# Issuing the loads and stores of the prepared weight sums from GpSimd, each load behind a copy from the newest low half of weights

## The chip, the cores and the metric

The kernel runs on one core of one Trainium2 chip. The metric is the device time of one execution in microseconds (us); the figure used is the median of several executions.

## The reference

One transformer layer on 256 tokens of width 2048, in fp32. Three attention branches are gated and mixed, then comes a feed-forward part, then a small gated input. Cut to what matters here:

```python
S, D = 256, 2048;  D_FF = 5632
z = split_cols(h @ w_in)                       # queries, keys, values, index queries, gates
o_fox = fox_attention(...)                     # 6 heads, forget-gated
o_nsa = nsa_attention(...)                     # 4 heads: compressed + selected blocks + window
o_dsa = dsa_attention(...)                     # 6 heads: an indexer picks 64 keys per query
g_fox, g_nsa, g_dsa = split(sigmoid(z['gate']), 3)
mixed = g_fox * (o_fox @ w_br_fox) + g_nsa * (o_nsa @ w_br_nsa) + g_dsa * (o_dsa @ w_br_dsa)
h = layer_norm(ALPHA * h + mixed @ w_out)
a, b = split(h @ w_ffn_in, 2)
h = layer_norm(ALPHA * h + (silu(a) * b) @ w_ffn_out)
h = h + (p @ w_ple_in) * sigmoid(h @ w_ple_gate)
```

## The kernel before

**Products in halves.** Each fp32 matrix is split into a high and a low half of a shorter type, and a product is three matmuls on TensorE: high by high, low by high, high by low (L244 to L246 in `gemm`; L297 to L299 in `pair_gemm`). `halves` (L156) makes the two: ScalarE writes the high half, VectorE subtracts it from the source and writes the low half. For weights the rows read `whi<-raw` and `wlo<-raw,whi`.

**Weight groups.** `gemm` streams a weight matrix in groups of up to 128x1024 elements (512 KB). SyncE issues the load of a group into one of three `raw` buffers, ScalarE and VectorE split it, TensorE uses it. Each instruction of these engines stands in an order of its own engine that is fixed when the program is built; an engine works through that order and waits at each row for what the row needs. `newest[0]` is, while the program is written down, the low half of the group written last.

**The attention stage** (0 to about 400 us) is written as the projections `c1` to `c7` and `f0` to `f5` of the input, 105 weight groups, with the small work of the heads between them. After each group `tick()` advances a few generators by a step: the heads (`dsa_head`, `nsa_head`, `fox_head`), the indexer (`index_scores`; its sums on VectorE are L744), and others. A step of a head is for instance `rope` (L542 to L546, on VectorE: tiles `ra` and `rb`), whose result TensorE transposes (`sc<-ident,ra`, L553), or `softmax` (L559 to L579): scores on TensorE, maximum on VectorE (L565), exponential on ScalarE (L567), reciprocal and scaling by VectorE (L570, L572, L574, tile `p`), transposition by TensorE (`sc<-ident,p`, L578). A scheduler then sets each engine's order from this program and its dependencies, so what is written between two groups need not stand between the same two.

**The prepared sums.** In the feed-forward product, `pair_gemm` replaces eight products of 2x2 blocks by seven, which takes sums of weight blocks. For seven pieces of the weight (two rows of tiles each), these sums are made early, in the attention stage, by `prepare` (L889 to L920), and kept in DRAM tiles `pre`, already split into halves. A piece ("job") takes two loads of 512 KB (tiles `preb` and `prea`, L898), four subtractions of 128x512 on VectorE (L900 to L904, tile `pret`), four splits into halves (L156), and five stores (L912, L913, L920). `pair_gemm` reads the tiles back from 928 us on. `prepare` runs on the ticks too, as three generators:

```python
PREPARED, PREPARE_FROM = (((4, 2), (5, 2)), ((6, 2), (7, 2), (8, 2)), ((9, 2), (10, 2))), 26
```

The first starts at tick 26 and takes one job there and one at tick 44; the other two start when the compressed values are done, and take two jobs at tick 57, two at 75 and one at 93. These five times are called batch 1 to 5 here: one, one, two, two and one jobs. The `yield 6` between the loads and the first subtraction leaves six ticks. The buffers of the three generators come from the pools `k4`, `gp` and `ka`, which the heads use as well.

**Queues.** All loads of weights and all loads and stores of `prepare` are issued by SyncE, in its order. GpSimd has 44 instructions: some copies and memsets (`blk`, L694, among them) and the loads of the norm parameters (`gb`, L1086). Its copies of one or two elements `...<-wlo` (L511, L1084) write a corner of a tile that is about to be loaded, so that the load cannot be issued before a given low half exists.

Of the kernel before, what the change touches and what calls it, by code (L numbers as in the profile page):

```python
# [10 lines left out]
F32 = mybir.dt.float32  # L11
# [117 lines left out]
def build(ctx: ExitStack, tc: tile.TileContext, A: dict):  # L129
    nc = tc.nc  # L130
    PE, DVE, ACT, POOL = nc.tensor, nc.vector, nc.scalar, nc.gpsimd
# [22 lines left out]
    def halves(src, hi, lo):  # L154

        split_last[:] = [ACT.activation(hi, src, AF.Copy).ins, DVE.tensor_sub(lo, src, hi.bitcast(F32)).ins]  # L156
# [18 lines left out]
    side, beside, now, newest = [], [], [0], [None]  # L175
# [285 lines left out]
    with ExitStack() as at:  # L461
# [429 lines left out]
        def prepare(jobs, pool, tag, after=None):  # L891

            while after and not T[after]["done"]:
                yield 1
            for c, p in jobs:
                rb, ra, t = (pool.tile([P, 2, 512], F32, name=f"pre{x}", tag=tag) for x in "bat")
                for r, n in ((rb, 11 + c), (ra, c)):
                    nc.sync.dma_start(r, A["ffn_in"][n][:, 2 * p:2 * p + 2, :])  # L898
                yield 6
                DVE.tensor_sub(t[:, 0, :], rb[:, 0, :], rb[:, 1, :])  # L900
                DVE.tensor_sub(t[:, 1, :], rb[:, 0, :], ra[:, 0, :])
                yield 1
                DVE.tensor_sub(rb[:, 1, :], rb[:, 1, :], t[:, 1, :])
                DVE.tensor_sub(ra[:, 1, :], ra[:, 1, :], rb[:, 1, :])  # L904
                yield 1
                for i, r in enumerate((rb, ra)):
                    halves(t[:, i, :], r[:, 0, :].bitcast(F32R), t[:, i, :].bitcast(F32R))
                    yield 1
                yield 1
                d = prepared.setdefault(c, {})[p] = dram.tile([P, 8, 512], F32, name="pre")  # L910
                for i, r in enumerate((rb, ra)):
                    nc.sync.dma_start(d[:, i:i + 1, :], r[:, 0:1, :])  # L912
                nc.sync.dma_start(d[:, 2:4, :], t)  # L913
                yield 3
                for r in (rb, ra):
                    halves(r[:, 1, :], r[:, 0, :].bitcast(F32R), r[:, 1, :].bitcast(F32R))
                    yield 1
                yield 1
                for i, r in enumerate((rb, ra)):
                    nc.sync.dma_start(d[:, 4 + 2 * i:6 + 2 * i, :], r)  # L920
                yield 1

        T = {}
        beside.append({"gen": prepare(PREPARED[0], k4, "k4"), "at": PREPARE_FROM})
        lf_task = add(later_load())
        ps = chunk("c1", x=X_first, sizes=[[1], [1]])
# [21 lines left out]
        for i, (pool, tag) in enumerate(((gp, "g"), (ka, "ka"))):  # L948
            beside.append({"gen": prepare(PREPARED[1 + i], pool, tag, "v"), "at": 0})
# [432 lines left out]
```

## Time and profile before

| | |
|---|---|
| median of 3 runs | 1564.12 us (1563.99 to 1565.78) |
| profiled execution | 1562.82 us, of which the span of its instructions 1560.9 us |
| TensorE matmul (PE) | 1545.5 us busy, 99% of the span |
| VectorE (DVE) | 1367.2 us, 88% |
| ScalarE (ACT) | 881.8 us, 56% |
| GpSimd (POOL) | 20.1 us, 1% |
| granted TensorE clock | full throughout |
| DMA | 360.91 MB, 231 GB/s over the span |

In the rows of the trace, PE is TensorE's matmuls, PEld its weight loads, DVE VectorE, ACT ScalarE, POOL GpSimd and SP SyncE. A row of the order of time has the start and the length of an instruction or a run of equal ones in us, the engine, the line, the operation, the tiles written and read (`out<-in`), the shape and the count; in brackets stands the idle time before it and what ended it. A row of waits has engine, tile and line that waited, what it waited for, then the idle time, the number of times and the longest. Rows of a tile have the instruction's duration in ns (smallest, median, largest) and the first and last start in us; the row under it the time from a DMA's issue to its landing.

### The profile page before, as it was taken

To read this page: it belongs to the slowest core of one execution; us is meant where nothing else is said; L and a number is where in the kernel's file an instruction comes from. 1 tells how busy PE (TensorE), PEld (TensorE's weight loads), DVE (VectorE), ACT (ScalarE), POOL (GpSimd) and SP (SyncE) were. 2 spreads that over 40 slices of the span, in tenths; PEclk is the share of its full clock that TensorE was granted. 3 is DMA by queue.
4 is the path that set the end of the run, shared out by engine and by line. 5 is a ranking of instruction groups with operands and counts; after the bars stand their busy time and mean duration, and the time that the engine had idled before them with its cause. 6 is when DMAs were issued, how large, how long until landed. Compare 5 with 4: busy or idle time off the path is not lost. (4 is left out here: it accounts for less than half of the span.)

```text
span 1560.9 us, 20529 instructions
## 1 busy us (share of the span) xinstructions
PE 1545.5 (99%) x7314; PEld 1286.8 (82%) x7314; DVE 1367.2 (88%) x1914; ACT 881.8 (56%) x1155; POOL 20.1 (1%) x44
## 2 busy tenths in 40 slices
PE   9999999999999999999999999999999999999998
PEld 7778899998888888888788888888888888887887
DVE  6779787559898998998879999999999999989896
ACT  5545566556565555544455566656565666555463
POOL 1000000000000000001000000000000000010000
PEclk9999999999999999999999999999999999999999
DMA  8866988566645664658566667777777776886554
GB/s 284 303 215 211 302 284 283 169 209 206 237 158 192 216 236 158 229 172 265 160 219 214 229 213 245 262 263 271 266 261 275 245 267 229 290 289 251 166 171 135
DMA packets 105574, 360.91 MB, mean 231 GB/s; under 512 B 12032, under 2 KB 13184, under 8 KB 105472
## 3 DMA queue, kind: packets, MB, share of 16 engines
q1 hardware_dynamic: 104192, 355.41, 67.2%
q0 software_dynamic: 1280, 4.20, 0.9%
q8 instruction: 57, 0.93, 0.2%
q14 instruction: 45, 0.37, 0.1%
HBM read 337.54 MB, written 22.02 MB: 230 GB/s over the span
## 5 line engine op out<-in xcount | busy, mean ns | idle before, releaser
L156 DVE TENSOR_TENSOR wlo<-raw,whi 128x1024 fp32r<-128x1024 f32 (+3 forms) x539 | 586.7, 1104 | 131.8 <-ACT whi L156 128.0
L156 ACT ACTIVATE whi<-raw 128x1024 fp32r<-128x1024 f32 (+3 forms) x539 | 507.5, 962 | 338.3 <-PE acc L245 99.5
L244 PE MATMUL acc<-whi,k4h 128*128 128x512 f32 (+3 forms) x724 | 274.2, 379 | 1.8 <-ACT k4h L156 1.5
L246 PE MATMUL acc<-wlo,k4h 128*128 128x512 f32 (+3 forms) x724 | 267.0, 370 | 1.1 <-DVE wlo L156 1.1
L245 PE MATMUL acc<-whi,k4l 128*128 128x512 f32 (+3 forms) x724 | 267.2, 369 | 0.6 <-DVE k4l L156 0.6
L156 ACT ACTIVATE wthi<-raw 128x1024 fp32r<-128x1024 f32 x168 | 177.8, 1060 | 149.7 <-DVE raw L380 80.8
L156 DVE TENSOR_TENSOR wtlo<-raw,wthi 128x1024 fp32r<-128x1024 f32 x168 | 202.7, 1219 | 0.0
L297 PE MATMUL sc<-whi,k4h 128*128 128x512 f32 x489 | 191.6, 392 | 0.0
L298 PE MATMUL sc<-whi,k4l 128*128 128x512 f32 x489 | 190.5, 390 | 0.0
L299 PE MATMUL sc<-wlo,k4h 128*128 128x512 f32 x489 | 190.2, 390 | 0.1
L297 PE MATMUL acc<-whi,k4h 128*128 128x512 f32 x401 | 157.4, 393 | 0.3 <-ACT whi L156 0.3
L299 PE MATMUL acc<-wlo,k4h 128*128 128x512 f32 x401 | 156.4, 390 | 0.9 <-DVE wlo L156 0.9
L244 PEld LDWEIGHTS acc<-whi,k4h 128*128 128x128 f32 x724 | 136.1, 188 | 25.7 <-issue 4.7
L298 PE MATMUL acc<-whi,k4l 128*128 128x512 f32 x401 | 156.1, 389 | 0.0
L246 PEld LDWEIGHTS acc<-wlo,k4h 128*128 128x128 f32 x724 | 135.9, 188 | 21.5 <-DVE wlo L156 3.0
L245 PEld LDWEIGHTS acc<-whi,k4l 128*128 128x128 f32 x724 | 136.3, 188 | 18.7 <-DVE k4l L156 1.3
L380 DVE TENSOR_TENSOR raw<-raw 128x1024 f32<-128x1024 f32 x79 | 96.3, 1220 | 14.5 <-DMA raw<-ffn_out 5.9
L299 PEld LDWEIGHTS sc<-wlo,k4h 128*128 128x128 f32 x489 | 91.8, 188 | 19.9 <-DVE wlo L156 0.5
L297 PEld LDWEIGHTS sc<-whi,k4h 128*128 128x128 f32 x489 | 91.9, 188 | 18.8
L298 PEld LDWEIGHTS sc<-whi,k4l 128*128 128x128 f32 x489 | 91.8, 188 | 18.8
L299 PEld LDWEIGHTS acc<-wlo,k4h 128*128 128x128 f32 x401 | 75.2, 188 | 17.6 <-DVE wlo L156 1.9
L297 PEld LDWEIGHTS acc<-whi,k4h 128*128 128x128 f32 x401 | 75.3, 188 | 15.8 <-ACT whi L156 0.7
(370 smaller groups left out, 2120.4 us busy)
## 6 DMA issues: line engine op xcount, KB each, us to landing
raw<-ffn_in SPq DMA_DIRECT2D x169, 512.0 KB, 4.6
raw<-gate SPq DMA_DIRECT2D x96, 512.0 KB, 4.5
raw<-ffn_out SPq DMA_DIRECT2D x88, 512.0 KB, 5.0
raw<-att_c SPq DMA_DIRECT2D x40, 512.0 KB, 4.7
raw<-att_f SPq DMA_DIRECT2D x48, 384.0 KB, 3.8
raw<-ple_gate SPq DMA_DIRECT2D x32, 512.0 KB, 4.2
g<-actd SPq DMA_DIRECT2D x20, 512.0 KB, 5.0
g<-cmp SPq DMA_DIRECT2D x16, 512.0 KB, 5.6
```

The costliest lines, as they stand in the source:

```text
L156: split_last[:] = [ACT.activation(hi, src, AF.Copy).ins, DVE.tensor_sub(lo, src, hi.bitcast(F32)).ins]
L244: PE.matmul(o, xh[:, c], h, start=(k == 0), stop=False)
L245: PE.matmul(o, xl[:, c], h, start=False, stop=False)
L246: PE.matmul(o, xh[:, c], l, start=False, stop=(k == kt - 1))
L297: PE.matmul(o, xh, h, start=first, stop=False)
L298: PE.matmul(o, xl, h, start=False, stop=False)
L299: PE.matmul(o, xh, l, start=False, stop=stop)
L380: DVE.tensor_tensor(t[0], raw[:, 0:1, :].broadcast_to([P, 2, 512]), raw[:, 1:3, :], op=ALU.subtract)
```

## The change

Each of the two loads of a job gets a copy of one element ahead of it on GpSimd: from the low half of the newest weight group into the corner of the tile to be loaded. The loads (L899 after the change) and the five stores (L913, L914, L921) are issued by GpSimd instead of SyncE. In the new file all lines from there on are one higher: the subtractions are L901 to L905.

```diff
             for c, p in jobs:
                 rb, ra, t = (pool.tile([P, 2, 512], F32, name=f"pre{x}", tag=tag) for x in "bat")
                 for r, n in ((rb, 11 + c), (ra, c)):
-                    nc.sync.dma_start(r, A["ffn_in"][n][:, 2 * p:2 * p + 2, :])
+                    POOL.tensor_copy(r[:1, 0, :1], newest[0].bitcast(F32)[:1, :1])
+                    nc.gpsimd.dma_start(r, A["ffn_in"][n][:, 2 * p:2 * p + 2, :])
                 yield 6
...
                 for i, r in enumerate((rb, ra)):
-                    nc.sync.dma_start(d[:, i:i + 1, :], r[:, 0:1, :])
-                nc.sync.dma_start(d[:, 2:4, :], t)
+                    nc.gpsimd.dma_start(d[:, i:i + 1, :], r[:, 0:1, :])
+                nc.gpsimd.dma_start(d[:, 2:4, :], t)
...
                 for i, r in enumerate((rb, ra)):
-                    nc.sync.dma_start(d[:, 4 + 2 * i:6 + 2 * i, :], r)
+                    nc.gpsimd.dma_start(d[:, 4 + 2 * i:6 + 2 * i, :], r)
                 yield 1
```

The scheduler orders each engine anew. On GpSimd, the rows between the corner copies of the constants and those of the norm parameters were, before:

```order
L511 COPY peT<-wlo 1x1
L511 COPY cmp_113<-wlo 1x1
L694 MEMSET blk_853 128x32x17
L694 MEMSET blk_1524 128x32x17
L1084 COPY gb<-wlo 1x2 x4
L1086 DMA gb<-ln_g 128x512
```

After the change the first batch reads (`preb` and `prea` are the two loaded tiles, `pret` the third, `pre` the tile in DRAM):

```order
L511 COPY cmp_113<-wlo 1x1
L898 COPY preb<-wlo 1x1
L898 COPY prea<-wlo 1x1
L899 DMA preb<-ffn_in 128x1024
L899 DMA prea<-ffn_in 128x1024
L913 DMA pre<-preb 128x512
L913 DMA pre<-prea 128x512
L694 MEMSET blk_855 128x32x17
L914 DMA pre<-pret 128x1024
L921 DMA pre<-preb 128x1024
L921 DMA pre<-prea 128x1024
```

The first memset now stands between the stores of batch 1. The other batches follow in the same pattern, in batches 3 and 4 with four copies, then four loads. The copies of the five batches read the low halves of weight groups 26, 44, 57, 75 and 93, counted from the first.

On VectorE, at the end of weight group 27 of the attention stage (batch 1), the order was, before, with the preparation's last low halves of this batch already behind it:

```order
L744 SCALAR_TENSOR_TENSOR work<-ri,zs,work 128x128
L744 SCALAR_TENSOR_TENSOR work<-ri,zs,work 128x256
L744 SCALAR_TENSOR_TENSOR work<-ri,zs,work 128x128
L744 SCALAR_TENSOR_TENSOR work<-ri,zs,work 128x256
L156 TENSOR_TENSOR wlo<-raw,whi 128x1024
```

and after:

```order
L744 SCALAR_TENSOR_TENSOR work<-ri,zs,work 128x128
L744 SCALAR_TENSOR_TENSOR work<-ri,zs,work 128x256
L901 TENSOR_TENSOR pret<-preb 128x512
L902 TENSOR_TENSOR pret<-preb,prea 128x512
L904 TENSOR_TENSOR preb<-preb,pret 128x512
L156 TENSOR_TENSOR wlo<-raw,whi 128x1024
```

The subtractions of batch 1 moved from groups 13 to 22 to groups 27 to 30, one group behind the low half that their loads' copies read.

At the last forget-gated heads (batch 5, groups 93 to 95) VectorE's order was, before:

```order
L156 TENSOR_TENSOR wlo<-raw,whi 128x768 x4
L868 SCALAR_TENSOR_TENSOR fb<-sc,cum,cst 128x128
L870 SCALAR_TENSOR_TENSOR fb<-sc,cum,cst 128x256
L156 TENSOR_TENSOR wlo<-raw,whi 128x768
L565 ISA p,nm<-sc,fb 128x128
L565 ISA nm 128x1
L565 ISA p,nm<-sc,fb 128x256
L565 ISA nm 128x1
L570 RECIPROCAL rr<-rs 128x2
L574 TENSOR_SCALAR p<-p,rr 128x128
L574 TENSOR_SCALAR p<-p,rr 128x256
```

and after:

```order
L156 TENSOR_TENSOR wlo<-raw,whi 128x768 x4
L868 SCALAR_TENSOR_TENSOR fb<-sc,cum,cst 128x128
L870 SCALAR_TENSOR_TENSOR fb<-sc,cum,cst 128x256
L901 TENSOR_TENSOR pret<-preb 128x512
L565 ISA p,nm<-sc,fb 128x128
L565 ISA nm 128x1
L565 ISA p,nm<-sc,fb 128x256
L565 ISA nm 128x1
L156 TENSOR_TENSOR wlo<-raw,whi 128x768
L570 RECIPROCAL rr<-rs 128x2
L902 TENSOR_TENSOR pret<-preb,prea 128x512
L574 TENSOR_SCALAR p<-p,rr 128x128
```

The first two subtractions, which stood after weight group 79 before, now stand ahead of the maximum (L565) and the scaling (L574) of a head's softmax. The order of batches 3 and 4 moved likewise: the first subtraction from group 56 to behind group 58, and from group 70 to behind group 76. In batch 2 it stays at group 48.

## Prediction, made before the changed kernel ran

> **What bounds the kernel now.** I read the page first: its busy times, then the same by stretches, then who waits for whom, then the order of time around the moved transfers. The span and the engine that fills it, from the page:
>
> ```profile
> span 1560.9 us, 20529 instructions
> PE 1545.5 (99%) x7314; PEld 1286.8 (82%) x7314; DVE 1367.2 (88%) x1914; ACT 881.8 (56%) x1155; POOL 20.1 (1%) x44
> ```
>
> TensorE is the bound: 15.4 us of the span are not its own. So the change can give back little, and costs whatever TensorE is made to wait. All loads and stores that move are issued between 28 and 270 us, in the attention stage. Busy time by stretches (the last two columns are the share of the DMA engines and GB/s):
>
> ```profile
> core 0: us, PE busy (x) PEld busy (x) DVE busy (x) ACT busy (x) POOL busy (x), PEclk, DMA share, GB/s
> 160.00:200.00 40.00, 39.87 (x263) 34.08 (x252) 30.23 (x74) 20.38 (x42) 0.00 (x0) 1.00 0.94 310
> 200.00:240.00 40.00, 38.29 (x229) 35.41 (x228) 32.38 (x94) 23.46 (x59) 0.00 (x0) 1.00 0.84 275
> 240.00:280.00 40.00, 38.22 (x229) 36.50 (x228) 26.80 (x65) 23.72 (x56) 0.00 (x0) 1.00 0.78 264
> ```
>
> TensorE's only losses here are 3.5 us between 200 and 280. Who ended its waits from 40 to 330 us (all rows, TensorE), and one row of VectorE's waits:
>
> ```profile
> PE sc L578 <- DVE p L574: 1.7, 2, 1.1
> PE sc L559 <- ACT fq L554: 1.0, 1, 1.0
> PE sc L553 <- ACT rf L859: 0.8, 1, 0.8
> PE sc L805 <- issue: 0.6, 1, 0.6
> DVE pret L900 <- DMA preb<-ffn_in: 3.8, 2, 2.1
> ```
>
> No row says that TensorE waited for a weight load, so taking transfers out of SyncE's queue has nothing to win there directly. The first and the last row belong together, as the order of time shows (VectorE, then TensorE):
>
> ```profile
> 224.74 0.69 DVE L900 TENSOR_TENSOR pret<-preb 128x512 f32<-128x512 f32 x1 [2.12 <-DMA preb<-ffn_in]
> 225.78 0.61 PE L578 MATMUL sc<-ident,p 128*128 128x128 f32 x3 [0.61 <-DVE p L574]
> ```
>
> VectorE works in order. It stood 2.12 us before a preparation subtraction whose load had not landed; the softmax scaling L574 queued behind came late, and TensorE lost 1.7 us in all. A preparation load that lands late is paid by TensorE, through whatever stands behind the subtraction on VectorE. This is the pattern that I look for in the changed order.
>
> **The change, part by part.** *SyncE loses 49 issues* (14 loads, 35 stores): worth nothing, by the waits above. *GpSimd gets 14 copies and 49 issues.* The only issues that it makes in the trace are the norm parameters, 256 KB each, eight in a row; of each second one the issue and its landing (us from its issue), and of the pair at 1369.8:
>
> ```profile
> 707.39 1.12 POOL L1084 COPY gb<-wlo 1x2 f32<-1x2 f32 x4 [598.56 <-DMA raw<-w_out]
> 708.46 0.71 POOL L1086 DMA_DIRECT2D gb<-ln_g  x1
> L1086 POOL DMA_DIRECT2D gb<-ln_b x1: 544/544/544, 709.2 to 709.2; - x1
> DMA to landing us min/median/max: 4.4/4.4/4.4
> L1086 POOL DMA_DIRECT2D gb<-ln_b x1: 536/536/536, 710.2 to 710.2; - x1
> DMA to landing us min/median/max: 6.0/6.0/6.0
> L1086 POOL DMA_DIRECT2D gb<-ln_b x1: 536/536/536, 711.3 to 711.3; - x1
> DMA to landing us min/median/max: 8.0/8.0/8.0
> L1086 POOL DMA_DIRECT2D gb<-ln_b x1: 541/541/541, 712.3 to 712.3; - x1
> DMA to landing us min/median/max: 9.1/9.1/9.1
> L1086 POOL DMA_DIRECT2D gb<-ln_b x1: 536/536/536, 1370.4 to 1370.4; - x1
> DMA to landing us min/median/max: 6.5/7.7/8.9
> ```
>
> GpSimd's own time, some 49 x 0.54 = 26 us and 14 copies, fits into an engine that is idle 99%. What counts is the landing. Counted from the first issue at 708.5, 512 KB had landed after 5.2 us, 1 MB after 7.8, 1.5 MB after 10.9, 2 MB after 13.0. I take these for preparation loads of 512 KB issued one behind the other, because they are the only ones from this queue. Before them come the copies, 1.1 us for four and some 0.7 for two. So after the low half that gates a batch: with two loads 5.9 and 8.5 us; with four 6.4, 9.0, 12.1 and 14.3.
>
> *The gate.* In the changed order the copies read the low halves of weight groups 26, 44, 57, 75 and 93 (two, two, four, four and two loads), and VectorE's first subtraction stands behind group 27, 48, 58, 76 and 94. Only at the second batch do four groups lie between; I cost that at nothing. At the others one group lies between, a few microseconds against 6 to 14. Before, SyncE issued ahead (the last pair at 250.9, of which the gate is now at 294.6). So VectorE will stand four times. The rows of before that give gate and deadline, in the order of the batches (VectorE, ScalarE, TensorE):
>
> ```profile
> 71.15 1.23 DVE L156 TENSOR_TENSOR wlo<-raw,whi 128x1024 fp32r<-128x1024 f32 x1 [0.59 <-ACT whi L156]
> 79.92 1.40 DVE L744 SCALAR_TENSOR_TENSOR work<-ri,zs,work 128x128 f32<-128x128 f32 x4
> 81.24 0.68 DVE L542 TENSOR_TENSOR ra<-acc,cst 128x512 f32<-128x512 f32 x1
> 84.25 0.60 PE L553 MATMUL sc<-ident,ra 128*128 128x128 f32 x4
> 86.24 1.00 DVE L695 TENSOR_TENSOR blk<-nsT,peT 128x480 f32<-128x480 f32 x1
> 182.70 0.69 DVE L900 TENSOR_TENSOR pret<-preb 128x512 f32<-128x512 f32 x1
> 183.30 0.69 DVE L903 TENSOR_TENSOR preb<-preb,pret 128x512 f32<-128x512 f32 x1
> 183.41 0.83 ACT L156 ACTIVATE whi<-raw 128x768 fp32r<-128x768 f32 x1
> 185.01 0.96 DVE L156 TENSOR_TENSOR wlo<-raw,whi 128x768 fp32r<-128x768 f32 x1
> 195.55 0.28 DVE L542 TENSOR_TENSOR ra<-acc,cst 128x128 f32<-128x128 f32 x1
> 197.18 0.27 PE L553 MATMUL sc<-ident,ra 128*128 128x128 f32 x1
> 244.81 0.95 DVE L156 TENSOR_TENSOR wlo<-raw,whi 128x768 fp32r<-128x768 f32 x1
> 254.60 0.49 PE L578 MATMUL sc<-ident,p 128*128 128x128 f32 x3
> 293.66 0.96 DVE L156 TENSOR_TENSOR wlo<-raw,whi 128x768 fp32r<-128x768 f32 x1 [1.12 <-ACT whi L156]
> 302.40 0.49 PE L578 MATMUL sc<-ident,p 128*128 128x128 f32 x3
> ```
>
> A subtraction of 128x512 takes 0.60 from start to start (182.70 to 183.30).
> - Batch 1, gate 72.4: the second load lands at 80.9. Behind it, in order, two subtractions (1.2), a low half (1.1), four index-score sums (1.4), half a rope (five operations from 81.24, 1.9): 86.5. TensorE transposes that rope at 84.25: 2.3 late. The blocks of L695 (86.24) need a GpSimd memset that now stands behind two of this batch's stores; the sum puts L695 at 88.5 anyway, and I count nothing more for it.
> - Batch 3: the gate was 186.0, but four preparation operations that stood ahead of it on VectorE are gone, and ScalarE's high half at 183.41 had itself waited for one. I take 184.2, the early end, since nothing else stands ahead. The fourth load lands at 198.5; behind it two subtractions, a low half of an attention output and half a small rope (2.3): 200.8. TensorE wants it at 197.18: 3.6 late.
> - Batch 4, gate 245.8 less one preparation operation, 245.2: the third load lands at 257.3, then a subtraction and the scaling L574 (1.1): 258.4 against 254.60, 3.8 late.
> - Batch 5, gate 294.6: the second load lands at 303.1, with the same 1.1 at 304.2 against 302.40, 1.8 late.
>
> That is 11.5 us. The wait of 1.7 us at 225 goes, because batch 4's subtractions no longer stand there: net +9.8. The other waits of TensorE in the list (ScalarE's rf and fq copies) I leave at what they are. The stores land on GpSimd's queue too, and ScalarE's second halves wait for them; weights are split ahead of use, so I take nothing, and up to 1 us a batch for the upper end.
>
> Against the profiled execution (1562.82 us, of which 1.9 lie outside the span) this makes 1572.6; the median of the runs, 1564.12, stands 1.3 above that execution, and the same sum on it gives 1573.9.
>
> *Bounds.* Below: if later loads follow at the 310 GB/s of the row at 160, 1.7 us apart, the four delays come to 1.5, 0.9, 1.5 and 0.9, net +3.1, 1567; if no load is late, -1.7, 1562.4. Above: the pair at 1369.8 landed 512 KB 9.5 us after its first issue (0.6 and 8.9) instead of 5.2; 4.3 more on each of four batches is +27, 1591. I take the eight in a row, as the batches are issued in a row too.
>
> The Trainium skill has a shorter landing: "DMA: Bandwidth & Descriptors", section on the anatomy of one DMA on the GpSimd path, fits 2.0 us plus bytes over 436 GB/s, by which (an estimate from that page) 512 KB land in 3.2 us and 2 MB in 6.8; by that sum no batch is late and the time is that of the second rival. The trace does not agree: 512 KB took 5.2 to 9.5.
>
> **The rivals.**
> - *Loads land in time, nothing is lost.* GpSimd's queue is its own, and the pieces of its transfers need not stand behind weight loads that SyncE issued earlier. Then the wait at 225 goes and nothing comes: 1562.4, no difference. For it: the smallest landing above, 4.4. Against it: the gap to cover at batches 4 and 5 is about one group, 2 to 3 us, and no landing is under 4.4. The Trainium skill's same page, in its section saying that issuing engines are not separate DMA queues, has all of them run on the same 16 engines, so that only issue time is saved; by that rule the landings would be those of before, and only the gate counts.
> - *Faster.* SyncE no longer holds weight loads behind stores that wait for ScalarE and VectorE, so high halves come earlier and the rf, fq and p waits go: at most the 4.1 us of the four TensorE rows, 1560.0. It decides only if every load of a batch also lands within the one group between gate and use; then VectorE never stands. Against it: TensorE had no wait for weights.
> - *Worse than the sum.* Landings like those at 1370, and ScalarE standing before its second halves because the stores are queued on GpSimd behind each other: 1586 and over.
>
> **How the numbers follow.** 0.2% is 3.1 us, about what a measurement of this kernel tells from no change: faster is under 1561.0, slower over 1567.2. The forecast has 0.66 (1567.2 to 1586), loads in time 0.18, faster 0.07, worse 0.09. So slower is 0.75, same 0.18, faster 0.07. I predict 1574, and 1562 to 1586 holds all but some 0.15. The slower cases alone run from 1568 to 1590.
>
> **What would show it.** Right: VectorE rows pret<-preb and pret<-preb,prea with an idle time of 2 us or more ended by a DMA at batches 1, 3, 4 and 5 and none at batch 2; TensorE rows that wait for rope and p from VectorE, some 11 us in sum; no loss after 330 us. Wrong: the same subtractions without idle time, or landings under 4 us. A VectorE that stands while TensorE does not would mean that I read the deadlines too tight.

## The result and the profile after

The changed kernel takes 1576.15 us against 1564.13 before (medians of six runs each, shared): ratio 1.0071, 95% interval 1.0052 to 1.0089. It is slower by 12.0 us, where 1574.0 was forecast. The profiled execution took 1576.78 us. One execution each of two kernels of the experiments took 4010 us and is left out of their times. From the page of the changed kernel:

```profile
span 1574.9 us, 20600 instructions
PE 1549.9 (98%) x7314; PEld 1287.7 (82%) x7314; DVE 1367.7 (87%) x1914; ACT 878.6 (56%) x1155; POOL 48.3 (3%) x107
```

The span is 14.0 us longer: TensorE is idle for 9.6 us more (25.0 instead of 15.4) and busy for 4.4 us more, though it has the same 7314 matmuls. VectorE and ScalarE have about as much work as before. The stretches shown before, and the next one (columns as there):

```profile
160.00:200.00 40.00, 38.57 (x250) 31.85 (x249) 25.84 (x56) 18.00 (x37) 5.92 (x14) 1.00 0.81 283
200.00:240.00 40.00, 39.09 (x234) 36.41 (x232) 32.12 (x100) 24.42 (x60) 4.82 (x9) 1.00 0.74 246
240.00:280.00 40.00, 38.72 (x227) 36.50 (x227) 28.25 (x67) 23.42 (x55) 7.97 (x18) 1.00 0.66 220
280.00:320.00 40.00, 36.66 (x216) 35.43 (x215) 23.16 (x43) 21.10 (x44) 3.70 (x9) 1.00 0.73 243
```

TensorE was full from 280 to 320 before (40.00) and now loses 3.3 us. The waits from 40 to 345 us: the first five of TensorE, all of VectorE for preparation loads, all of ScalarE for preparation stores:

```profile
PE sc L553 <- ACT rf L859: 2.6, 2, 2.1
PE sc L578 <- DVE p L574: 2.4, 3, 1.3
PE sc L553 <- DVE ra L546: 1.7, 2, 1.1
PE sc L559 <- ACT fq L554: 1.6, 1, 1.6
PE sc L783 <- DMA g<-cmp: 1.3, 1, 1.3
DVE pret L901 <- DMA preb<-ffn_in: 7.5, 5, 3.4
DVE pret L901 <- issue: 1.7, 1, 1.7
DVE pret L902 <- DMA prea<-ffn_in: 1.3, 2, 0.7
ACT preb L156 <- DMA pre<-preb: 6.6, 2, 3.4
ACT prea L156 <- DMA pre<-prea: 1.3, 1, 1.3
```

VectorE's stand before `pret<-preb` grew from 3.8 us to 9.2 (7.5 and 1.7; the row of 1.7 names no releaser, and stands before the first subtraction of batch 3). The two rows of ScalarE are a second kind of stand. The second split of a job writes its high half where the first one lies, so it has to wait until the store of the first has landed.

Where TensorE lost its time is seen when the start of each weight group's first matmul is compared in the two traces. The delay after minus before, in us:

| from group to group | delay | step | what lies there |
|---|---|---|---|
| 1 to 26 | 0 to 2.5 | +2.5 | no preparation yet |
| 26 to 27 | 2.5 to 3.8 | +1.3 | batch 1, loads |
| 48 to 51 | 3.9 to 5.5 | +1.6 | batch 2, second halves; TensorE waits for `g<-cmp` |
| 56 to 59 | 5.5 to 6.0 | +0.5 | batch 3, loads |
| 59 to 70 | 6.0 to 4.8 | -1.2 | 1.3 lost up to group 69; 2.5 won at 70, behind the wait at 225 of before |
| 74 to 76 | 4.8 to 6.6 | +1.8 | batch 4, loads |
| 93 to 94 | 6.8 to 8.4 | +1.6 | batch 5, loads |
| 98 to 100 | 8.4 to 12.3 | +3.9 | batch 5, second halves; then half clock |

At group 121, 374 us into the trace of before, the delay is still 12.3; the last 1.7 us of the 14.0 come later, spread. Batch 5 shows both stands (GpSimd, VectorE, ScalarE and TensorE in order of time):

```profile
301.52 0.17 POOL L898 COPY preb<-wlo 1x1 f32<-1x1 f32 x1 [24.24 <-DVE wlo L156]
302.04 0.53 POOL L899 DMA_DIRECT2D preb<-ffn_in  x1 [0.23 <-POOL prea L898]
307.54 0.69 DVE L901 TENSOR_TENSOR pret<-preb 128x512 f32<-128x512 f32 x1 [3.35 <-DMA preb<-ffn_in]
310.66 0.61 PE L578 MATMUL sc<-ident,p 128*128 128x128 f32 x3 [1.27 <-DVE p L574]
316.00 0.63 ACT L156 ACTIVATE preb<-preb 128x512 fp32r<-128x512 f32 x1 [3.40 <-DMA pre<-preb]
323.54 0.84 ACT L156 ACTIVATE whi<-raw 128x768 fp32r<-128x768 f32 x1 [3.49 <-DMA raw<-att_f]
324.69 0.63 PE L553 MATMUL sc<-ident,rf 128*128 128x128 f32 x2 [2.13 <-ACT rf L859]
```

The copy runs as soon as the low half is there, the load is issued 0.5 us later, and VectorE stands 3.35 us for it. The maximum of the head's softmax waits behind, and TensorE gets its `p` 1.27 us late. That chain was forecast. The next was not: ScalarE stands 3.40 us for a store, and the halves behind it are late. The weight load of group 101 is issued at 318.38, as soon as the low half of group 98 has freed its buffer; counted from the delay of 8.4 us that TensorE has there, that is 3.2 us later than before (306.76). It also takes 5.0 us to land instead of 3.4. TensorE waits 2.13 us for the `rf` that stands behind this group's high half on ScalarE.

That wait is only a part of the step of 3.9. From 324.81 to 328.22 the granted TensorE clock is 0.5, as the column PEclk of these stretches shows, and the same matmul takes longer (two rows of TensorE, before and in it):

```profile
324.00:326.00 2.00, 1.30 (x6) 1.31 (x7) 0.96 (x1) 0.92 (x4) 0.00 (x0) 0.70 0.65 258
326.00:328.00 2.00, 2.00 (x8) 2.00 (x7) 1.23 (x3) 1.27 (x3) 0.00 (x0) 0.50 0.63 187
320.44 0.33 PE L246 MATMUL acc<-wlo,k4h 128*128 128x384 f32 x1
326.19 0.52 PE L246 MATMUL acc<-wlo,k4h 128*128 128x384 f32 x1
```

Such matmuls start 0.32 us apart there instead of 0.17. Half the clock for 3.4 us is some 1.7 us of lost work (an estimate from these two numbers); with the wait of 2.13 it makes the step of 3.9. The trace of before has no such stretch within its span.

### The profile page after: what moved, and what is told of

Read it like the earlier page. It is cut to its first block, busy times and chain, and to the rows that moved or that the text cites. A ratio compares the mean times of both kernels' runs of the same rounds, so it can differ in the third digit from the quotient of the medians.

```text
span 1574.9 us, 20600 instructions
## 1 busy us (share of the span) xinstructions
PE 1549.9 (98%) x7314; PEld 1287.7 (82%) x7314; DVE 1367.7 (87%) x1914; ACT 878.6 (56%) x1155; POOL 48.3 (3%) x107
## 4 chain that ended last, share of the span: by engine, by line
PE 75%; DMA 8%; issue 7%; DVE 7%; ACT 2%; POOL 1%; SPq 0%; ACTq 0%; DVEq 0%; POOLq 0%
PE sc L299 9%; PE sc L298 9%; PE sc L297 9%; PE acc L299 9%; PE acc L297 9%; PE acc L298 9%; PE acc L244 5%; PE acc L246 5%; PE acc L245 5%; DVE wlo L156 3%; DMA raw<-att_c 2%; DMA raw<-w_out 2%; DMA preb<-ffn_in 2%; ACT whi L156 2%; PE sc L246 1%
```

## The experiments

All ratios are against the kernel before, timed beside them.

**Taking the stands away.** Ties put rows later on VectorE and ScalarE; nothing else in the program changes, though the scheduler orders it anew. There are three kernels: first only the subtractions, then also the second halves, then only the second halves.

```diff
                 yield 6
-                DVE.tensor_sub(t[:, 0, :], rb[:, 0, :], rb[:, 1, :])
-                DVE.tensor_sub(t[:, 1, :], rb[:, 0, :], ra[:, 0, :])
+                with tc.issue_after(split_last[1]):
+                    DVE.tensor_sub(t[:, 0, :], rb[:, 0, :], rb[:, 1, :])
+                    DVE.tensor_sub(t[:, 1, :], rb[:, 0, :], ra[:, 0, :])
...
                 for r in (rb, ra):
-                    halves(r[:, 1, :], r[:, 0, :].bitcast(F32R), r[:, 1, :].bitcast(F32R))
+                    with tc.issue_after(split_last[0]), tc.issue_after(split_last[1]):
+                        halves(r[:, 1, :], r[:, 0, :].bitcast(F32R), r[:, 1, :].bitcast(F32R))
```

The first edit alone:

> The changed kernel, but the first two subtractions of each job are tied behind the low half of the weight group at which they are written: they stand at groups 32, 50, 63, 81 and 99 instead of 27, 48, 58, 76 and 94, five or six groups behind their gates. Theory (VectorE stands before a subtraction whose load was issued one group earlier): no row of VectorE waits for preb or prea, TensorE's steps at groups 27, 57, 76 and 94 go (1.3, 0.6, 1.1 and 1.6 us in the trace of the changed kernel), the wait of ScalarE for its first store may stay: 1568 to 1572. Rival (GpSimd's queue and its traffic delay the weight loads, whoever waits for the preparation): 1575 to 1577, nothing gained.

Measured: 1567.17, ratio 1.0018 (1.0006 to 1.0030), a little better than expected. VectorE has no wait for a preparation load any more, so the rival falls. ScalarE's stand for stores is as long as in the changed kernel:

```profile
ACT preb L156 <- DMA pre<-preb: 7.0, 3, 3.0
```

But the second halves have moved along, behind groups 33, 51, 68, 86 and 102 (counted by the low halves on VectorE), and there no step of TensorE is over 0.4 us.

Both edits:

> As the kernel with held subtractions, and the second halves of each job are tied behind the weight group at which they are written, some seven groups behind the stores that they wait for. Theory (ScalarE too stands, 3.4 us at batch 5, before a second half whose store has not landed, and TensorE lost 3.9 us at groups 99 and 100 by it): ScalarE's waits for the store go as well, 1564 to 1568, about 4 under the kernel with held subtractions alone. Rival (the 3.9 us come from late weight loads by themselves): no gain over that kernel.

Measured: 1565.55, ratio 1.0010 (0.9999 to 1.0021). No stand for preparation loads or stores is left, and of the 0.71% at most 0.2% remains. The median is 1.6 us below that of the first edit alone, not 4, and the two intervals overlap.

The second edit alone:

> The changed kernel with its subtractions where they are, and only the second halves tied seven groups behind the stores. Theory (at batch 5 ScalarE's stand of 3.4 us for a store, and the weight loads behind it, cost TensorE 3.9 us): groups 99 and 100 lose nothing, the four steps of VectorE stay: 1570 to 1573. Rival (the stores' waits are hidden, all goes back to VectorE's waits): 1575 to 1577.

Measured: 1569.26, ratio 1.0026 (1.0012 to 1.0039), less than expected. The steps at groups 51, 99 and 100 are gone, and VectorE's stands are all there:

```profile
DVE pret L901 <- DMA preb<-ffn_in: 6.8, 3, 3.1
DVE pret L902 <- DMA prea<-ffn_in: 2.0, 3, 0.9
```

So the rival that all goes back to VectorE's waits falls: the second halves were worth about as much as the loads. The trace also tells a late issue from a slow landing: the weight load of group 101 still takes 5.2 us to land, but it is issued at 313.83, only 0.7 us later than before when the delay of 6.4 is taken off, and TensorE loses nothing there. The two gains (0.53% and 0.45%, 8.3 and 7.0 us) do not add up, since holding the subtractions moves the second halves too.

**The distance from gate to subtraction.** The tie of the first edit with two, then three ticks instead of six; the ticks are given back at the end of the job.

```diff
-                yield 6
+                yield 2
                 with tc.issue_after(split_last[1]):
...
                     nc.gpsimd.dma_start(d[:, 4 + 2 * i:6 + 2 * i, :], r)
-                yield 1
+                yield 5
```

> The kernel with held subtractions, tied two groups behind the gate instead of six (the ticks taken away there are given back at the end of the job): the subtractions stand at groups 28, 47, 59, 77 and 95, about where the kernel with copies and SyncE has them. Theory (distance between gate and subtraction): part of the waits is back, 1569 to 1573, between the changed kernel and the one with six groups. Rival (not the distance but GpSimd's queue makes the loads late, so that these places cost on GpSimd what the changed kernel costs): 1574 to 1577. If the places alone mattered, it would be near the 1567.7 of SyncE with copies.

Measured: 1576.51, ratio 1.0074 (1.0053 to 1.0094): nothing gained, the rival's number. But the rival's mechanism is not what the trace shows: the loads land in a median of 5.7 and 7.0 us, a little later than in the changed kernel (5.2 and 6.7). VectorE still stands 6.9 us (3.5 and 3.4 in its two rows, 10.5 in the changed kernel), ScalarE nearly as long as there (7.2), and TensorE waits more for `p`. The two longest of these waits, 2.65 us at 259.77 and 2.04 at 310.63, each have a stretch of 3.4 us at half clock beside them:

```profile
PE sc L578 <- DVE p L574: 6.3, 4, 2.6
```

> As before with three groups: 29, 47, 60, 78 and 96. Theory: the waits of VectorE for one pair are gone and those for two pairs (10 to 11 us for four loads) are small: 1567 to 1570. Rival: no change against two groups.

Measured: 1574.71, ratio 1.0061 (1.0043 to 1.0079), a miss. VectorE's stand is all but gone, as the theory says, but ScalarE's has taken its place, since the second halves (behind groups 32, 50, 67, 82 and 98, counted as above) now follow the later subtractions and stores more closely:

```profile
DVE pret L903 <- DMA prea<-ffn_in: 0.8, 2, 0.6
DVE pret L902 <- DMA preb<-ffn_in: 0.4, 1, 0.4
ACT preb L156 <- DMA pre<-preb: 11.6, 3, 4.3
```

Groups 98 to 101 lose 4.2 us in its trace, with a stretch of 3.4 us at half clock from 326.34. The distance to the loads alone is thus not the cause; one stand was traded for the other.

**The parts of the change.** Only the loads with their copies on GpSimd, the stores back on SyncE:

```diff
-                    nc.gpsimd.dma_start(d[:, i:i + 1, :], r[:, 0:1, :])
-                nc.gpsimd.dma_start(d[:, 2:4, :], t)
+                    nc.sync.dma_start(d[:, i:i + 1, :], r[:, 0:1, :])
+                nc.sync.dma_start(d[:, 2:4, :], t)
...
-                    nc.gpsimd.dma_start(d[:, 4 + 2 * i:6 + 2 * i, :], r)
+                    nc.sync.dma_start(d[:, 4 + 2 * i:6 + 2 * i, :], r)
```

> Loads on GpSimd behind their copies as in the changed kernel, stores issued by SyncE as before; VectorE's preparation stands in the same groups as in the changed kernel. Theory (the gate ahead of the loads costs the time): as the changed kernel, 1572 to 1578. Rival (the stores on GpSimd's queue cost it): 1564 to 1568.

Measured: 1573.06, ratio 1.0062 (1.0048 to 1.0077). VectorE's order is the same as in the changed kernel up to group 97, and the steps are much the same: 2.0 at group 27, 2.2 at group 94, 4.2 at 99 and 100 (again with 3.4 us at half clock, from 321.69). That is as the theory said, and the rival falls: ScalarE stands 5.1 us for stores that SyncE issues, and the loss stays. So it does not need the stores on GpSimd.

The copies kept, and all loads and stores issued by SyncE:

```diff
                     POOL.tensor_copy(r[:1, 0, :1], newest[0].bitcast(F32)[:1, :1])
-                    nc.gpsimd.dma_start(r, A["ffn_in"][n][:, 2 * p:2 * p + 2, :])
+                    nc.sync.dma_start(r, A["ffn_in"][n][:, 2 * p:2 * p + 2, :])
```

with the stores as in the edit above.

> The copies of the changed kernel stay, but loads and stores are all issued by SyncE again; VectorE's subtractions stand at groups 27, 48, 58, 77 and 95. Theory (the short way from gate to subtraction costs the time, and the queue only who else is held): VectorE waits for preb or prea as in the changed kernel, and SyncE, which now holds weight loads behind each gated load, adds a little: 1573 to 1582. Rival (the queue of GpSimd lands later, and that is the cost): 1564 to 1568.

Measured: 1567.74, ratio 1.0018 (1.0007 to 1.0028): the theory, which put the whole loss on the gate, is wrong by 5 us or more, and the rival's time came. Its places on VectorE and those of the second halves are within a group of the kernel with two groups (1.0074), so without cover a small difference is worth 0.56%: VectorE stands 5.3 us for loads here, 6.9 there. But the rows within these groups differ too (in batch 4 the first subtraction of the second job stands behind the scaling L574 here, ahead of it there), and there are stretches at half clock there and none here. So the issuer and the order are not separated. The DMAs from 60 to 345 us, KB and median us from issue to landing, in the changed kernel:

```profile
preb<-ffn_in POOLq DMA_DIRECT2D x7, 512.0 KB, 5.2
prea<-ffn_in POOLq DMA_DIRECT2D x7, 512.0 KB, 6.7
pre<-preb POOLq DMA_DIRECT2D x7, 512.0 KB, 8.3
pre<-preb POOLq DMA_DIRECT2D x7, 256.0 KB, 3.8
```

and with copies on SyncE, with its only wait of ScalarE for a store:

```profile
preb<-ffn_in SPq DMA_DIRECT2D x7, 512.0 KB, 5.6
prea<-ffn_in SPq DMA_DIRECT2D x7, 512.0 KB, 6.4
pre<-preb SPq DMA_DIRECT2D x7, 512.0 KB, 6.0
pre<-preb SPq DMA_DIRECT2D x7, 256.0 KB, 2.4
ACT prea L156 <- DMA pre<-prea: 2.8, 1, 2.8
```

The loads land alike, so this rival's mechanism, later landings of the loads, is not shown. The stores of these two rows land 1.4 and 2.3 us later from GpSimd, but that is not a property of the issuer alone: in the other kernels the median of the 512 KB store of `preb` is 5.4 to 7.3 us from GpSimd (eight kernels), and 4.6 to 6.5 from SyncE (five, with this one). That of `prea` is 6.2 to 7.8 from GpSimd and 4.7 to 6.2 from SyncE. What makes the difference these runs do not show.

Only the stores on GpSimd, the loads without copies on SyncE:

> Loads issued by SyncE without copies as before, only the stores on GpSimd. Theory (the gate on the loads costs the time): as the kernel before, 1561 to 1566. Rival (stores on GpSimd cost it): 1570 and over.

Measured: 1578.97, ratio 1.0094 (1.0078 to 1.0111), a clear miss. SyncE now waits, between weight loads, for stores that another engine issues; the waits of SyncE's queue from 203 to 256 us, and its issues at the second of two such places:

```profile
SPq L898 <- DMA pre<-preb: 7.2, 2, 7.0
SPq L898 <- DMA pre<-pret: 5.6, 2, 4.3
244.40 0.33 SPq L898 DMA_DIRECT2D preb<-ffn_in  x1
251.75 0.33 SPq L898 DMA_DIRECT2D prea<-ffn_in  x1
252.17 0.85 SPq L168 DMA_DIRECT2D raw<-att_f  x1
```

The load of `prea` has to wait until an earlier job's store out of its buffer has landed, 7.0 us, and a weight load stands behind it. VectorE stands 3.2 us for this `prea`, and 4.1 us are lost at groups 73 and 74. The first place is dearer: SyncE stands 4.3 us before a load of `prea` at 213.97, and groups 66 and 67 lose 6.1. At both, TensorE waits over 2 us for `p` (2.23 at 223.85, 2.41 at 258.04), and the clock is at half for 6.8 and 3.4 us. So this part alone costs about as much as the whole change or more (the intervals overlap).

Loads and stores on GpSimd, without the copies:

> Loads and stores on GpSimd as in the changed kernel, without the copies; the subtractions stand at groups 9, 48, 56, 67 and 76, near those of the kernel before. Theory (gate): most of the loss goes, 1564 to 1569; some stays at groups 66 and 67, where a load waits for stores of its buffers that land 8 to 12 us after their issue on GpSimd. Rival (GpSimd's queue alone costs it): 1573 to 1579, as with the stores alone on GpSimd.

Measured: 1582.48 (three executions), ratio 1.0112 (1.0092 to 1.0132), a miss again. The first load goes out at 1.31 us, among the kernel's first weight loads, and the loads of a later batch stand behind stores in GpSimd's order. The last line is the landing of the two loads at 218.29:

```profile
1.31 0.69 POOL L898 DMA_DIRECT2D preb<-ffn_in  x1 [0.44 <-issue]
215.65 0.53 POOL L920 DMA_DIRECT2D pre<-prea  x1 [0.56 <-ACT whi L156]
216.29 0.55 POOL L898 DMA_DIRECT2D preb<-ffn_in  x1
218.29 1.08 POOL L898 DMA_DIRECT2D prea<-ffn_in  x2 [1.46 <-DMA pre<-preb]
prea<-ffn_in POOLq DMA_DIRECT2D x2, 512.0 KB, 12.3
```

By group 19 this trace is 8.6 us late, and groups 66 and 67 lose another 7.5; each of the two includes waits of TensorE over 2.5 us (3.53 at 60.78, 2.53 at 229.47) and 6.8 us at half clock. That the early loads and the place behind the stores are what makes these waits is argued from the order, not shown apart. In this order the copies on GpSimd are no cost but a gain.

**With both held, who issues?** The same places on VectorE in all three: SyncE without copies (the kernel before with the two edits), GpSimd without copies, and GpSimd for gated loads with the stores on SyncE.

> The kernel before (SyncE, no copies) with the subtractions and the second halves tied as in the kernel with both held: groups 32, 50, 63, 81, 99. Theory (waits of VectorE and ScalarE for the preparation are what moves the time, on either queue): the wait of 1.7 us at 225 goes, 1561 to 1564. Rival (the later places themselves cost, or SyncE's stores hold weight loads): 1566 and over.

> The kernel with both held, without the copies: the same places on VectorE, loads issued on GpSimd as soon as their buffers are free. Theory (once five groups lie between gate and use, the gate costs nothing): the same as with the copies, 1564 to 1567. Rival (the gate still costs): 1561 to 1563.

> The kernel with both held, stores issued by SyncE again: only gated loads on GpSimd. Theory (with cover the queue of the stores costs little): 1563 to 1566, as the kernel before or the one with both held. Rival (stores on GpSimd were what kept that one above the kernel before): 1561 to 1563.

Measured: 1563.45, ratio 0.9991 (0.9980 to 1.0002); 1567.29, 1.0013 (1.0002 to 1.0024); 1565.57, 0.9999 (0.9988 to 1.0011). The first and the last are within their theories, the second 0.3 us above. With the 1.0010 of gate and queue of the changed kernel, both held, the four lie within 0.22%: with cover, gate and queue are worth little (by the ends of the intervals at most 0.44%). None of the kernels is measurably faster than the one before.

## Why the prediction was right, and where not

The direction and the kind of mechanism were right: preparation that is not ready stops an engine that works in order, and TensorE pays. That the time came so near (1574 against 1576.15) is luck, because the terms were not right and their errors cancelled: in the trace the loads cost 5.2 us instead of 11.5, and the stores 5.5 instead of nothing.

- *VectorE's four stands.* They are there, at batches 1, 3, 4 and 5 and not at 2, as read from the order, though the longest is under the forecast 2 us at batches 1 and 3 (0.8 and 1.7). The landings were right too: in batch 4, 5.2, 8.0, 9.7 and 10.9 us after the first issue, against 5.2, 7.8, 10.9 and 13.0. The cost was over-sized: 1.3, 0.5, 1.8 and 1.6 us against 2.3, 3.6, 3.8 and 1.8. The worst step is batch 3, where I let the last of four loads stop everything. The subtractions of its second job stand later in the order, and TensorE had its rope 0.5 us late.
- *"The stores ... I take nothing, and up to 1 us a batch for the upper end."* This step failed. Second halves that wait for stores cost 1.6 us at batch 2 and 3.9 at batch 5 in the trace (1.7 of the 3.9 by the half clock), and holding them alone took 0.45%, 7.0 us, off the time. I had argued that weights are split ahead of use. But a late split frees its weight buffer late, the next load is issued late, and ScalarE's copy of `rf` stands behind the split that waits for it. At batch 2 the load of `g<-cmp` stands on SyncE behind a weight load that waits for such a buffer. The stand is not longer than before: in the trace of before ScalarE waited 8.2 us for stores (two rows, of which the longer is below), after the change 7.9. It now lies where TensorE has no slack.

```profile
ACT preb L156 <- DMA pre<-preb: 4.7, 3, 2.8
```

- *The clock.* The forecast has no term for it; it counts a late instruction at its lateness. In the fourteen traces, TensorE waits 2.0 us or more eleven times after the start, and ten of these waits have a stretch of 3.4 or 6.8 us at half clock beside them. Few of the shorter waits have one. The executions differ in this: the mean granted clock is 0.9988 over the six of the changed kernel and 0.9990 to 0.9994 over those of the kernel before, so over all executions such stretches make less than 1 us of the 12.0 (an estimate: 0.06% of 1576 us), though 1.7 in this trace.
- *The wait at 225.* It went: between 205 and 245 us TensorE waits 0.3 us for `p` instead of 1.7, and the delay falls by 1.2 from group 59 to 70.
- *Nothing before the first gate.* The trace is 2.5 us late by then. Nine of the kernels run here have the same order on ScalarE, VectorE and SyncE up to group 20, and are -0.3 to 2.7 us late there, so a difference of this size lies within the scatter between executions and is not shown to be the change.
- *Not separated.* The forecast blames the gate with the queue's landings. Copies with loads and stores on SyncE cost 0.18%, a quarter of the loss, but in that kernel the subtractions of batches 4 and 5 stand one group later as well. With loads alone on GpSimd, in VectorE's order of the changed kernel, nearly all of the loss is there (0.62%). How much of the rest is the issuer of the loads and how much the order stays open.
- *The rival that loads land in time* had the Trainium skill on its side: "DMA: Bandwidth & Descriptors", section on issuing engines not being separate DMA queues, has only issue time saved by a second issuer. For loads the traces agree (5.2 and 6.7 us from GpSimd, 5.6 and 6.4 from SyncE), and with cover the four times agree as well. For stores they are mixed (5.4 to 8.3 us for `preb` from GpSimd, 4.6 to 6.5 from SyncE).
- The Trainium skill's fit on the same page, by which 512 KB take an estimated 3.2 us, is not seen: the fastest median of GpSimd's loads here is 5.2. By that fit no batch is late, which is the time of the first rival (1562.4) and not, as the forecast says, of the second. The forecast's landings for four loads are 0.1 to 0.2 us above their own sum, which changes nothing.

## What to carry to other kernels

When a load is gated, look where the in-order engine that uses it has its first use: the distance from gate to use must cover the landing (here some 11 us for four loads of 512 KB), and a scheduler that moves the use up can undo the distance that the program text shows. Then look for the next wait of the same kind, a store that must land before its buffer is written again; giving the loads three groups only moved the loss there. Before a store is put on another queue than the loads, look for a load that must wait for it: where weight loads stood behind such a load on SyncE, the stores alone cost 0.94%, while moving only the loads cost no more than moving both. And when you price a wait of the matmul engine, look at the granted clock behind it: here a wait of 2.13 us cost 3.9.

## What had not been expected of the hardware

A wait of some 2 us was followed by TensorE at half clock for 3.4 us, with matmuls 0.32 us apart instead of 0.17. The two slowest kernels have the lowest mean granted clock over their executions: 0.9958 with only the stores on GpSimd and 0.9953 with loads and stores there without copies, where the kernel before, timed beside them, has 0.9994. That is worth some 6 us of losses of 14.7 and 17.5 (an estimate: these differences, of 1575 us).

Taking the gate away made things worse: the same queue without copies was 0.4% slower than with them. There the loads start among the kernel's first weight loads or behind stores, and a burst of stores and loads on GpSimd took long to land (10.4 us for a store and 12.3 for two loads at 215 to 219 us). With both edits the copies made no measurable difference (1.0013 without, 1.0010 with).
